# A GLA / S5 trunk on one core: GpSimd's elementwise work moved to VectorE, Toeplitz blocks read from the kernel table, low halves of the output weights by accumulating DMA

## The chip, the cores and the metric

The kernel runs on one core of a Trainium2 chip. The metric is device microseconds (us) of one execution. Five engines run their own instruction queues in order: TensorE (PE; its weight loads are shown as PEld), VectorE (DVE), ScalarE (ACT), GpSimd (POOL) and SyncE (SP), which here only issues DMAs. They meet through semaphores.

## The reference, cut to what matters

Two layers over x (512 tokens by 1024), each `x <- x + Mixer(RMSNorm(x))`, all in float32:

```
layer 0, GLA:  q,k,v,z,r = h @ w_in ; 4 heads, chunked, decay from sigmoid(r @ w_gate_up + b)
               o = attention inside the chunks + running state
               out = (rmsnorm_head(o) * silu(z)) @ w_out
layer 1, S5:   u,z = h @ w_in ; 128 groups of 16 channels, 64 complex states per group
               lam_bar = exp(lam*dt), b_bar = (lam_bar-1)/lam * b ; x_t = lam_bar*x_(t-1) + b_bar u_t
               y = gelu(Re(C x) + d*u) ; y = y*sigmoid(y @ w_glu + b_glu) * silu(z) ; out = y @ w_out
final RMSNorm
```

What S5's matrices hold is computed on the chip: for every group the powers of `lam_bar`, `b_bar` and C give a block Bm (inputs of 8 steps into the state), a block Cm (state into 8 outputs), a table E that rotates the states, and the short kernel K[0..7] (16 by 16 each), from which a lower Toeplitz block of 8 by 8 taps per group is laid out.

## The kernel before, in words

Every dense product is done in three matmuls on a high and a low half: weight and activation are split into `hi` (rounded for the fast fp32 mode) and `lo = value - hi`, and `three` adds hi*hi, hi*lo and lo*hi. A weight unit is 128 partitions by 1024 floats (512 KB); 136 units pass through the kernel, each feeding 24 matmuls of 128x512. `wunit` (L178) makes one unit. SP loads `raw` (two buffers, tag wraw). Then, of eight buffers of tag whl, four pairs, one pair is filled in one of two ways:

- plain: ACT copies raw to `hi` (L161), and DVE, or POOL where the table `UNITP` says so, subtracts (L162);
- with `dma=True`: ACT copies raw to `hi` (L185) and minus raw, rounded, to `lo` (L186), and POOL issues a DMA that adds the weight from HBM to `lo` (L187). It is used for w_z, w_qk and w_v of heads 1 to 3. w_out goes the plain way, all 16 units on DVE.

The GLA layer runs head by head (loop at L637). Of head h: `proj_qk`, then a weave of `proj_v`, `proj_out` of the head before (w_out) and `proj_z`, with the attention's steps `scores`, `state` and `mix` put between the units. Beside it runs S5Prep, which computes S5's matrices for 16 blocks of 8 groups. Its steps are called by `hook` from a list `plan`, at a pace `RATES`, each put off by `LOWS[step]` places of priority:

- F (`compute`, L1285): on POOL, ten elementwise operations per block: L1293, L1302 and L1304 on 128x1024, L1294 to L1297 on 128x512, L1309 to L1311 on 128x128 (and their inputs `lp`, `bb`, `xc`, `pp` loaded by SP, L1276 to L1282); then on DVE z = z + z2 (L1323) and the split of Bm into two fp16 halves (L1317 on ACT, L1318 on DVE), stored to HBM (L1319);
- Z (`finish_z`, L1326): the same split for Cm (z); PE computes the short kernel from z and bh (L1333); ACT and DVE evacuate (L1337, L1339), POOL adds the skip term and splits to fp16 (L1342 to L1345); SP stores it to the table `kz` in HBM (L1346); then `gcopy` (L1349) copies the block two before from `kz`, with overlapping strides, to the expanded Toeplitz matrix `gmd` (HBM to HBM, 512 KB);
- E (`etab`, L1250): a table by six operations on 128x512, the first three tables on DVE, the last five on POOL; G: the last `gcopy`.

S5's layer (L721 on) takes for each block sT, sR, sA, sB, sC and s5, scheduled by the tables TS to SGS, between the weight units of `win` (w_u, w_z, first of w_glu). `load_a` and `load_b` fetch Bm, E, the Toeplitz block and Cm with one DMA each (two each for the first three blocks). In sA POOL multiplies the scan's result (L812), in s5 POOL multiplies the gate with y (L847). 39 weight units there are plain, 23 of them subtracted on POOL. The last stretch, three quarters of w_glu and all of w_out of S5, is plain on ACT and DVE.

A scheduler builds each engine's queue from these priorities with its own estimate of durations; at run time each queue is strictly in order.

## Time and profile before

| | us |
|---|---|
| three runs | 1053.78, 1055.71, 1055.98 (median 1055.71) |
| profiled execution | 1054.56 |
| its span, first to last instruction | 1052.9 |
| PE busy | 927.6 (88%) |
| DVE busy | 713.8 (68%) |
| POOL busy | 511.0 (49%) |
| ACT busy | 472.2 (45%) |

The 1.7 us between span and time lie outside of the instructions. The busy share of an engine is an average over four stretches that differ: start and head 0 (to about 150 us), heads 1 to 3 with S5Prep beside them (150 to 550), S5 blocks between weight units (550 to 800), and weight units alone (from 800). A stretch is read by its own row. "Granted clock" (PEclk) is TensorE's clock as a share of full speed.

### The profile page before, as it was taken

To read this page: it belongs to the slowest core of one execution; us is meant where nothing else is said; L and a number is where in the kernel's file an instruction comes from. 1 tells how busy PE (TensorE), PEld (TensorE's weight loads), DVE (VectorE), ACT (ScalarE), POOL (GpSimd) and SP (SyncE) were. 2 spreads that over 40 slices of the span, in tenths; PEclk is the share of its full clock that TensorE was granted. 3 is DMA by queue.
4 is the path that set the end of the run, shared out by engine and by line. 5 is a ranking of instruction groups with operands and counts; after the bars stand their busy time and mean duration, and the time that the engine had idled before them with its cause. 6 is when DMAs were issued, how large, how long until landed. Compare 5 with 4: busy or idle time off the path is not lost. (4 is left out here: it accounts for less than half of the span.)

```text
span 1052.9 us, 13715 instructions
## 1 busy us (share of the span) xinstructions
PE 927.6 (88%) x5019; PEld 720.8 (68%) x5019; DVE 713.8 (68%) x916; ACT 472.2 (45%) x707; POOL 511.0 (49%) x477
## 2 busy tenths in 40 slices
PE   6795966699869796969989999999998999999996
PEld 5573754457646684747777777787777888888885
DVE  5794569957898887978645769789897432424322
ACT  5553343445546455433556684744453332313222
...
GB/s 256 221 183 100 87 167 185 276 247 262 265 209 250 228 292 273 237 321 317 190 226 259 151 121 250 211 300 252 264 185 140 110 82 99 100 160 100 100 61 80
DMA packets 118707, 205.79 MB, mean 195 GB/s; under 512 B 32400, under 2 KB 69824, under 8 KB 118640
## 3 DMA queue, kind: packets, MB, share of 16 engines
...
HBM read 167.69 MB, written 45.59 MB: 203 GB/s over the span
## 5 line engine op out<-in xcount | busy, mean ns | idle before, releaser
L162 DVE TENSOR_TENSOR whl<-wraw,whl 128x1024 fp32r<-128x1024 f32 x77 | 106.6, 1384 | 147.5 <-ACT whl L161 147.3
L161 ACT CAST whl<-wraw 128x1024 fp32r<-128x1024 f32 x100 | 104.7, 1048 | 183.7 <-PE pt L199 46.0
L202 PE MATMUL pd<-whl,actA 128*128 128x512 f32 x384 | 154.6, 408 | 12.9 <-ACT whl L161 9.2
L203 PE MATMUL pd<-whl,actA 128*128 128x512 f32 x384 | 154.2, 402 | 0.0
L204 PE MATMUL pd<-whl,actA 128*128 128x512 f32 x384 | 154.0, 404 | 0.0
L270 POOL TENSOR_TENSOR rstd<-rv,neghalf 128x1 f32<-128x1 f32 (+1 forms) x6 | 5.2, 874 | 248.4 <-DVE rv L269 248.4
L198 PE MATMUL pd<-actA,whl 128*128 128x512 f32 x256 | 101.6, 403 | 3.3 <-ACT u L732 3.1
L200 PE MATMUL pd<-actA,whl 128*128 128x512 f32 x256 | 101.4, 397 | 0.0
L202 PEld LDWEIGHTS pd<-whl,actA 128*128 128x128 f32 x384 | 74.4, 194 | 32.7 <-ACT whl L161 9.2
L202 PE MATMUL pd<-whl,q 128*128 128x512 f32 x192 | 80.3, 419 | 11.7 <-DVE xx L541 5.1
L204 PEld LDWEIGHTS pd<-whl,actA 128*128 128x128 f32 x384 | 73.9, 193 | 18.6 <-issue 2.8
L203 PEld LDWEIGHTS pd<-whl,actA 128*128 128x128 f32 x384 | 73.9, 192 | 17.7 <-issue 2.1
L162 POOL TENSOR_TENSOR whl<-wraw,whl 128x1024 fp32r<-128x1024 f32 x23 | 58.3, 2533 | 52.5 <-ACT whl L161 49.2
L203 PE MATMUL pd<-whl,q 128*128 128x512 f32 x192 | 79.6, 415 | 0.0
L1318 DVE TENSOR_TENSOR q<-q,q 128x1024 f16<-128x1024 f32 x32 | 60.4, 1886 | 12.6 <-ACT q L1317 12.3
L198 PEld LDWEIGHTS pd<-actA,whl 128*128 128x128 f32 x256 | 48.5, 190 | 16.6 <-ACT u L732 5.2
L1293 POOL TENSOR_TENSOR q<-q,q 128x1024 f32<-128x1024 f32 x16 | 43.4, 2709 | 31.7 <-DMA q<-s_bi 29.6
L198 PE MATMUL po<-actA,whl 128*128 128x512 f32 x128 | 52.4, 409 | 5.8 <-ACT whl L185 5.8
L185 ACT CAST whl<-wraw 128x1024 fp32r<-128x1024 f32 x36 | 37.7, 1046 | 44.0 <-PE pd L203 26.4
L200 PEld LDWEIGHTS pd<-actA,whl 128*128 128x128 f32 x256 | 48.4, 189 | 11.2
L204 PE MATMUL pd<-whl,q 128*128 128x512 f32 x128 | 53.7, 424 | 1.4 <-DVE q L165 1.4
L202 PEld LDWEIGHTS pd<-whl,q 128*128 128x128 f32 x192 | 38.4, 200 | 23.6 <-DVE xx L541 6.4
...
## 6 DMA issues: line engine op xcount, KB each, us to landing
wraw<-w_glu SPq DMA_DIRECT2D x32, 512.0 KB, 3.4
wraw<-w_v SPq DMA_DIRECT2D x16, 512.0 KB, 5.4
wraw<-w_z SPq DMA_DIRECT2D x16, 512.0 KB, 6.5
whl<-w_z POOLq DMA_DIRECT2D x16, 512.0 KB, 7.9
wraw<-w_out SPq DMA_DIRECT2D x16, 512.0 KB, 6.8
q<-lpt SPq DMA_DIRECT2D x16, 512.0 KB, 6.8
q<-s_bi SPq DMA_DIRECT2D x16, 512.0 KB, 9.5
...
```

The costliest lines, as they stand in the source:

```text
L161: i0 = A.copy(out=dst_hi, in_=src)
L162: i1 = E.tensor_tensor(out=dst_lo, in0=src, in1=f(dst_hi), op=SUB)
L185: A.copy(out=hi, in_=raw)
L198: PE.matmul(acc, lhsT=wh, rhs=ah, start=first, stop=False)
L200: mark["pe"] = PE.matmul(acc, lhsT=wl, rhs=ah, start=False, stop=last).ins
L202: PE.matmul(acc, lhsT=ah, rhs=wh, start=first, stop=False)
L203: PE.matmul(acc, lhsT=ah, rhs=wl, start=False, stop=False)
L204: mark["pe"] = PE.matmul(acc, lhsT=al, rhs=wh, start=False, stop=last).ins
L270: G.tensor_tensor(out=dst, in0=v, in1=neghalf.to_broadcast([P, w]), op=ALU.pow)
L1293: tt(out=m, in0=lp, in1=bb, op=MUL)
L1318: nc.vector.tensor_tensor(out=hl[:, 1], in0=src, in1=hl[:, 0], op=SUB)
```

## The change

Three things, and two tables that go with them (`LOWS`: F 0 to 30, Z 20 to 30; `UNITP` and `EV` are gone).

1. All elementwise work of POOL named above goes to DVE: `compute`, the end of `finish_z`, `etab`, L812, L847 and the 23 subtractions of weight units. On POOL stay the set-up (`small`), 16 small memsets of sR, the powers of RMSNorm and the DMA issues.
2. `gcopy` and `gmd` are gone. A Toeplitz block is read by eight DMAs, one per group (`toep`), each of 16x8 rows of 512 bytes, straight from `kz`.
3. w_out of the GLA layer is loaded with `dma=True`.

```diff
-LOWS = {'F': 0, 'Z': 20, 'E': 100, 'G': 0}
+LOWS = {'F': 30, 'Z': 30, 'E': 100}
...
-            E = V
-            if pool:
-                E = G if UNITP[wcnt[0]] else V
-                wcnt[0] += 1
-            mark["act"], mark["dve"] = split(hi, lo, raw, E=E)
+            mark["act"], mark["dve"] = split(hi, lo, raw)
...
-            yield from dense_tok(w_out[h, n], o[0], o[1], ev, per_tb=True)
+            yield from dense_tok(w_out[h, n], o[0], o[1], ev, per_tb=True, dma=True)
...
+        if src is prep.kz:
+            for g in range(GB):
+                S.dma_start(out=w[g // 4][:, g % 4 * 2 * P:(g % 4 + 1) * 2 * P], in_=prep.toep(cb * GB + g))
...
-        G.tensor_tensor(out=t1, in0=sh, in1=co, op=MUL)
+        V.tensor_tensor(out=t1, in0=sh, in1=co, op=MUL)
...
-        G.tensor_tensor(out=sz[cb], in0=sz[cb], in1=yv[cb], op=MUL)
+        V.tensor_tensor(out=sz[cb], in0=sz[cb], in1=yv[cb], op=MUL)
...
     def etab(self, ck):
-        tt = (nc.vector if ck < EV else nc.gpsimd).tensor_tensor
+        tt = nc.vector.tensor_tensor
...
     def compute(self, cb):
-        G = self.nc.gpsimd
-        tt = G.tensor_tensor
+        tt = self.nc.vector.tensor_tensor
...
-        G.tensor_tensor(out=dk, in0=self.dm, in1=self.kd[:, cb:cb + 1].to_broadcast([P, 16]), op=MUL)
-        G.tensor_tensor(out=ke[:, 0:16], in0=ke[:, 0:16], in1=dk, op=ADD)
-        G.tensor_copy(out=kf[:, :, 0], in_=ke)
-        G.tensor_tensor(out=kf[:, :, 1], in0=ke, in1=kf[:, :, 0], op=SUB)
+        V.tensor_tensor(out=dk, in0=self.dm, in1=self.kd[:, cb:cb + 1].to_broadcast([P, 16]), op=MUL)
+        V.tensor_tensor(out=ke[:, 0:16], in0=ke[:, 0:16], in1=dk, op=ADD)
+        V.tensor_copy(out=kf[:, :, 0], in_=ke)
+        V.tensor_tensor(out=kf[:, :, 1], in0=ke, in1=kf[:, :, 0], op=SUB)
...
-    def gcopy(self, cb):
-        src = bass.AP(self.kz.tensor, self.kz[cb * GB].offset + 7 * 32, [[2 * KW, P], [-32, T], [1, 2 * P]])
-        self.nc.sync.dma_start(out=self.gmd[cb].rearrange("g (i j) w -> (g i) j w", j=T), in_=src)
+    def toep(self, g):
+        return bass.AP(self.kz.tensor, self.kz[g].offset + 7 * 32, [[2 * KW, 16], [-32, T], [1, 2 * P]])
```

Lines of the changed kernel stand 3 to 19 lower (L1285 `compute` is L1273 on, L1333 is L1320, L161 in `split` is L158 and L164 is L161). How the queues come out of the scheduler is seen at three places.

First, ACT's queue at the start of head 1 in the kernel before. whl are weight tiles (here w_out), big_1230 to big_1233 the four token blocks of v, which the next state and mix matmuls on PE read, q_246 the first Bm:

```order
L161 CAST big_1277<-pt_1273 128x128
L164 ACTIVATE q_199_1188<-pt_1183,hgp 128x128 x2
L161 CAST big_1329<-pt_1325 128x128
L161 CAST whl_1524<-wraw_1522 128x1024
L161 CAST whl_1605<-wraw_1603 128x1024
L161 CAST big_1338<-pt_1334 128x128
L164 ACTIVATE big_1230<-pd_1238,rstd_77_513 128x512
L164 ACTIVATE big_1231<-pd_1239,rstd_77_513 128x512
L164 ACTIVATE big_1232<-pd_1240,rstd_77_513 128x512
L164 ACTIVATE big_1233<-pd_1241,rstd_77_513 128x512
L161 CAST whl_1675<-wraw_1673 128x1024
L1317 CAST q_246_1387<-q_205_1206 128x1024
```

The same place in the changed kernel, where big_1229 and the following are v:

```order
L180 CAST whl_1606<-wraw_1604 128x1024
L181 ACTIVATE whl_1607<-wraw_1604 128x1024
L161 ACTIVATE q_199_1187<-pt_1182,hgp 128x128
L158 CAST big_1276<-pt_1272 128x128
L180 CAST whl_1677<-wraw_1675 128x1024
L181 ACTIVATE whl_1678<-wraw_1675 128x1024
L161 ACTIVATE q_199_1187<-pt_1182,hgp 128x128 x2
L158 CAST big_1328<-pt_1324 128x128
L1304 CAST q_261_1450<-q_207_1212 128x1024
L158 CAST big_1337<-pt_1333 128x128
L161 ACTIVATE big_1229<-pd_1237,rstd_77_512 128x512
L161 ACTIVATE big_1230<-pd_1238,rstd_77_512 128x512
```

In the kernel before, the second and third units of w_out stand ahead of v; in the changed one all four do, with two operations each (the first two units stand a few rows above this piece, with q_246's cast), and two casts of S5Prep.

Second, DVE's queue at the end of head 1's gate projection (L396 and L398 gate the head's output, tile big; L433 and L438 belong to the next head's decay), before:

```order
L396 SCALAR_TENSOR_TENSOR tmp_1962<-tmp_1962,pd_1739 128x512
L398 SCALAR_TENSOR_TENSOR big_1556<-tmp_1958,rsv_1843,big_1556 128x512
L396 SCALAR_TENSOR_TENSOR tmp_1966<-tmp_1966,pd_1740 128x512
L398 SCALAR_TENSOR_TENSOR big_1579<-tmp_1962,rsv_1843,big_1579 128x512
L398 SCALAR_TENSOR_TENSOR big_1710<-tmp_1966,rsv_1843,big_1710 128x512
L433 TENSOR_SCALAR tmp_1976<-pt_1974,bg 128x512
L396 SCALAR_TENSOR_TENSOR tmp_1970<-tmp_1970,pd_1741 128x512
```

and in the changed kernel, where L386 and L388 are those operations and L1281 to L1289 are `compute`:

```order
L386 SCALAR_TENSOR_TENSOR tmp_1963<-tmp_1963,pd_1741 128x512
L1281 TENSOR_TENSOR q_412_2153<-q_413_2154 128x8x64
L1289 TENSOR_TENSOR q_414_2160<-big_1953,pp_1954 128x1024
L388 SCALAR_TENSOR_TENSOR big_1557<-tmp_1959,rsv_1845,big_1557 128x512
L386 SCALAR_TENSOR_TENSOR tmp_1967<-tmp_1967,pd_1742 128x512
L388 SCALAR_TENSOR_TENSOR big_1580<-tmp_1963,rsv_1845,big_1580 128x512
L1282 TENSOR_TENSOR q_413_2154<-q_368_1951,q_369_1952 128x8x64
L1283 TENSOR_TENSOR q_413_2154<-q_368_1951,q_369_1952 128x8x64
```

Operations of `compute` now stand one or two at a time between those of the head.

Third, SP's queue where S5 loads a block (number 4 of 16), before:

```order
L581 DMA q_1017_5268<-bmd 128x2048
L581 DMA q_1018_5270<-tab 128x1024
L581 DMA q_1019_5272<-gmd 128x8x256
L581 DMA q_1020_5274<-cmd 128x2048
```

and in the changed kernel:

```order
L570 DMA q_1017_5285<-bmd 128x2048
L570 DMA q_1018_5287<-tab 128x1024
L565 DMA q_1019_5289<-kz 128x1x256 x8
L570 DMA q_1020_5298<-cmd 128x2048
```

One DMA has become eight.

## Rows read from the trace of the kernel before

**Rows 1.** Stretches: start:end and length, each engine's busy us (x instructions), PEclk, DMA, GB/s.
```profile
150.00:550.00 400.00, 329.21 (x1413) 245.39 (x1413) 322.00 (x333) 187.53 (x296) 336.51 (x285) 0.90 0.88 253
550.00:800.00 250.00, 234.51 (x1997) 188.29 (x1996) 204.46 (x250) 137.74 (x192) 96.99 (x66) 0.98 0.68 218
800.00:1053.00 253.00, 244.21 (x1111) 196.40 (x1110) 90.08 (x106) 74.52 (x101) 8.97 (x8) 0.99 0.32 100
```

**Rows 2.** Two shorter stretches, the same columns.
```profile
700.00:750.00 50.00, 47.00 (x455) 38.37 (x454) 47.80 (x53) 20.52 (x30) 20.79 (x18) 1.00 0.81 261
850.00:1025.00 175.00, 175.00 (x754) 140.93 (x752) 59.37 (x64) 49.68 (x63) 0.00 (x0) 1.00 0.33 103
```

**Rows 3.** Waits of PE, 150 to 550 us: sum, times, longest.
```profile
PE pt L1333 <- DVE q L1323: 12.3, 2, 6.5
PE pt L1333 <- POOL bh L1311: 7.6, 2, 5.4
```

**Rows 4.** DVE's groups by form, 150 to 550 us.
```profile
L1318 DVE TENSOR_TENSOR q<-q,q 128x1024 f16<-128x1024 f32 x32 | 60.4, 1886 | 12.6 <-ACT q L1317 12.3
L162 DVE TENSOR_TENSOR whl<-wraw,whl 128x1024 fp32r<-128x1024 f32 x18 | 33.4, 1857 | 11.2 <-ACT whl L161 11.2
L1323 DVE TENSOR_TENSOR q<-q,q 128x1024 f32<-128x1024 f32 x16 | 30.2, 1891 | 0.0
L398 DVE SCALAR_TENSOR_TENSOR big<-tmp,rsv,big 128x512 f32<-128x512 f32 x12 | 24.1, 2038 | 0.0
L541 DVE TENSOR_TENSOR xx<-pd,xx 128x512 f32<-128x512 f32 x32 | 21.7, 680 | 4.4 <-PE pd L204 4.4
L174 DVE SCALAR_TENSOR_TENSOR big<-big,ges,big 128x512 fp32r<-128x512 f32 x9 | 18.5, 2052 | 0.1
L535 DVE TENSOR_TENSOR rsv<-rsv,rstd 128x4 f32<-128x4 f32 x3 | 11.2, 3749 | 3.1 <-POOL rsv L270 3.1
```

**Rows 5.** DVE's groups by form, 850 to 1025 us.
```profile
L162 DVE TENSOR_TENSOR whl<-wraw,whl 128x1024 fp32r<-128x1024 f32 x32 | 39.2, 1226 | 115.9 <-ACT whl L161 115.9
```

**Rows 6.** DVE in order of time: start, us, operation.
```profile
148.98 0.28 DVE L171 TENSOR_TENSOR big<-att,big 128x128 fp32r<-128x128 f32 x1
...
151.20 0.69 DVE L1260 TENSOR_TENSOR q<-big,big 128x512 f32<-128x512 f32 x1
151.80 0.68 DVE L1263 TENSOR_TENSOR q<-big,big 128x512 f32<-128x512 f32 x1
```

**Rows 7.** POOL's groups by form, 150 to 550 us.
```profile
L1293 POOL TENSOR_TENSOR q<-q,q 128x1024 f32<-128x1024 f32 x16 | 43.4, 2709 | 31.7 <-DMA q<-s_bi 29.6 <-issue 1.7 <-DMA tab<-q 0.4
L1297 POOL TENSOR_TENSOR q<-q 128x512 f32<-128x512 f32 x16 | 27.4, 1710 | 0.1
L1311 POOL TENSOR_TENSOR bh<-bh,bh 128x128 f32<-128x128 f32 x16 | 14.7, 920 | 0.1
```

**Rows 8.** The accumulating DMAs (L187): issue min/median/max ns, then landing us.
```profile
L187 POOL DMA_DIRECT2D whl<-w_v x12: 866/894/1948, 87.4 to 386.9; - x12
...
DMA to landing us min/median/max: 5.3/7.9/11.9
```

**Rows 9.** ACT in order of time at the start of head 1.
```profile
159.24 1.04 ACT L161 CAST whl<-wraw 128x1024 fp32r<-128x1024 f32 x1 [8.48 <-DMA wraw<-w_out]
...
162.53 2.43 ACT L164 ACTIVATE big<-pd,rstd 128x512 fp32r<-128x512 f32 x4
```

**Rows 10.** PE in order of time at the start of head 1.
```profile
163.28 1.22 PE L202 MATMUL po<-big,big 128*128 128x512 f32 x2 [11.08 <-ACT big L164]
169.34 0.80 PE L202 MATMUL pd<-whl,q 128*128 128x512 f32 x1 [4.84 <-DVE big L165]
```

**Rows 11.** SP's issues in order of time there.
```profile
118.24 0.33 SPq L180 DMA_DIRECT2D wraw<-w_out  x1
...
144.75 4.63 SPq L966 DMA_DIRECT2D kz<-tmp  x9
...
152.38 0.85 SPq L180 DMA_DIRECT2D wraw<-w_out  x2
```

**Rows 12.** DMAs: KB each, median us from issue to landing.
```profile
wraw<-w_out SPq DMA_DIRECT2D x16, 512.0 KB, 6.8
q<-gmd SPq DMA_DIRECT2D x13, 512.0 KB, 5.3
kz<-tmp SPq DMA_DIRECT2D x16, 56.0 KB, 1.9
```

More of the change, by code (lines that the diff above doesn't have):

```diff
@@ L58 @@
 LOW1, LOW2 = 20, 0
-EV = 3
 SCP = -20
@@ L157, in trunk_kernel, with split @@
     mark = {}
-    def split(dst_hi, dst_lo, src, scale=None, E=V):
+    def split(dst_hi, dst_lo, src, scale=None):
         if scale is None:
             i0 = A.copy(out=dst_hi, in_=src)
-            i1 = E.tensor_tensor(out=dst_lo, in0=src, in1=f(dst_hi), op=SUB)
+            i1 = V.tensor_tensor(out=dst_lo, in0=src, in1=f(dst_hi), op=SUB)
         else:
@@ L204, in three, with dense_tok @@
             mark["pe"] = PE.matmul(acc, lhsT=al, rhs=wh, start=False, stop=last).ins
-    def dense_tok(w, ah, al, evac, per_tb=False, late=True, major=1, pool=False, banks=None, dma=False):
+    def dense_tok(w, ah, al, evac, per_tb=False, late=True, major=1, banks=None, dma=False):
         nkb = 4 if per_tb else len(ah)
@@ L222, in fetch @@
         def fetch(u):
-            return wunit(w[u], 2, 512, pool=pool, dma=dma)
+            return wunit(w[u], 2, 512, dma=dma)
         for u in range(nu - major + 1):
@@ L245, in dense_tok, with dense_ch @@
                 yield
-    def dense_ch(w, ah, al, evac, pool=False, banks=None):
+    def dense_ch(w, ah, al, evac, banks=None):
         nkb = len(ah)
@@ L250, in dense_ch @@
         for u in range(nkb // 2):
-            hi, lo = wunit(w[u], 2, 512, pool)
+            hi, lo = wunit(w[u], 2, 512)
             for m in range(4):
@@ L364, in trunk_kernel @@
             ne += 1
-    plan.append(("G", NB - 1))
     pace = [0.0]
@@ L567, in loadw @@
         n = 1024 if dt == F16 else 512
-        if src is prep.gmd:
-            srcs = [src[cb, 4 * k:4 * k + 4].rearrange("g p w -> p g w") for k in range(2)]
-            full = src[cb].rearrange("g p w -> p g w")
-        else:
-            srcs = [src[cb][:, k * n:(k + 1) * n] for k in range(2)]
-            full = src[cb]
-        fit = (lambda t: t.rearrange("p (g w) -> p g w", w=2 * P)) if src is prep.gmd else (lambda t: t)
         if cb < NPRE:
             w = [T_([P, n], "big", BIG, dt) for _ in range(2)]
-            for k in range(2):
-                S.dma_start(out=fit(w[k]), in_=srcs[k])
-            return w
-        t = q4(dt, 2 * n)
-        S.dma_start(out=fit(t), in_=full)
-        return [t[:, :n], t[:, n:]]
+        else:
+            t = q4(dt, 2 * n)
+            w = [t[:, :n], t[:, n:]]
+        if src is prep.kz:
+            for g in range(GB):
+                S.dma_start(out=w[g // 4][:, g % 4 * 2 * P:(g % 4 + 1) * 2 * P], in_=prep.toep(cb * GB + g))
+        elif cb < NPRE:
+            for k in range(2):
+                S.dma_start(out=w[k], in_=src[cb][:, k * n:(k + 1) * n])
+        else:
+            S.dma_start(out=t, in_=src[cb])
+        return w
     def wsel(w):
@@ L597, in load_b @@
         t = st_[cb]
-        t["gh"] = gsel(loadw(cb, prep.gmd))
+        t["gh"] = gsel(loadw(cb, prep.kz))
         t["cm"] = wsel(loadw(cb, prep.cmd))
@@ L866, in win @@
             if c[0] == "u":
-                yield from dense_tok(s_wu[n], h2, l2, lambda tb, acc, n=n: ev_u(n, tb, acc), late=False, pool=True)
+                yield from dense_tok(s_wu[n], h2, l2, lambda tb, acc, n=n: ev_u(n, tb, acc), late=False)
             elif c[0] == "z":
-                yield from dense_ch(s_wz[n], h2, l2, lambda m, acc, n=n: ev_z(4 * n + m, acc), pool=True)
+                yield from dense_ch(s_wz[n], h2, l2, lambda m, acc, n=n: ev_z(4 * n + m, acc))
             else:
-                yield from dense_ch(w_glu[n], yh, yl, lambda m, acc, n=n: ev_g(4 * n + m, acc), pool=True)
+                yield from dense_ch(w_glu[n], yh, yl, lambda m, acc, n=n: ev_g(4 * n + m, acc))
     jobs = {}
@@ L948, in __init__ @@
         self.cmd = dr.tile([NB, P, 2 * GB * P], F16, name="cmd")
-        self.gmd = dr.tile([NB, GB, P, 2 * P], F16, name="gmd")
         self.tab = dr.tile([NB, P, 2 * GB * NC], F32, name="tab")
```

10 lines of the change are left out of this document (1 added, 9 removed).

## The prediction

> **What bounds the kernel now.** I read the table of stretches first, looking in each for the engine that is hardly ever idle [rows 1]. From 800 us on PE works 244.2 of 253 us and POOL 9.0; the change finds next to nothing there. From 550 to 800 PE works 234.5 of 250, so 15.5 us are all that can be won. From 150 to 550 PE works 329.2 of 400: 70.8 us idle, with DVE at 322.0 (80.5%) and POOL at 336.5 (84%). The granted clock there is 0.90, against 0.98 and 0.99 later. So the change is decided in heads 1 to 3 with S5Prep beside them; before 150 us it touches little.
>
> Second, PE's waits there. No single one carries the idle time. Two go back to S5Prep's chain: the short-kernel matmul waits 12.3 us for DVE and 7.6 for POOL [rows 3]. The longest pair is at the start of head 1, 11.08 + 4.84 = 15.9 us [rows 10]: PE wants v from ACT, and ACT had waited 8.48 us for a raw unit of w_out before it came to v's splits at 162.53 [rows 9]. SP had issued that raw load only at 152.38, behind nine small stores [rows 11].
>
> Third, DVE's groups. An operation on two 128x1024 inputs in SBUF takes 1226 ns where POOL does nothing [rows 5] and 1857 to 1891 ns where POOL is at work; the three-input 128x512 ones take 2038 and 2052, and a 128x4 one 3749. L541, with one input in PSUM, takes 680, like a free 128x512 record of 0.69 [rows 4, 6]. So DVE's 322 us hold much time in which it waits for POOL.
>
> **DVE in the 150 to 550 stretch.** What goes: POOL's elementwise work, and with it the stretching. From [rows 4] less the free prices: 32 x (1.886 - 1.226) = 21.1; 18 x (1.857 - 1.226) = 11.4; 16 x (1.891 - 1.226) = 10.6; 12 x (2.038 - 0.69) = 16.2; 9 x (2.052 - 0.69) = 12.3; 3 x (3.749 - 0.28) = 10.4, with 0.28 for a small record [rows 6]. Together 82. Smaller groups must have some too; I take 100, within 82 and 120 (an estimate).
>
> The w_out subtractions leave DVE: 16 x 1.14 = 18. Here and below I count operations back to back: 128x512 records of 0.69 start 0.60 apart [rows 6], so 0.09 overlaps; that makes 1.14 of 1.226, and 0.20 of 0.28.
>
> What comes: F, per block three operations of 1.14, four of 0.60 and three of 0.20, 6.4 us, x16 = 103. Four small ones of `finish_z`, 0.8, x15 = 12. E, five tables of six operations, 30 x 0.60 = 18. Four weight units, 4.6. Together 137.
>
> DVE then has 322 + 137 - 18 - 100 = 341 us, 85% of 400 (321 to 360 by the bounds). What took POOL 2709, 1710 and 920 ns an operation [rows 7], 336.5 / 16 = 21 us per block with all else [rows 1], takes DVE 1.14, 0.60 and 0.20, some 8. How full can DVE run before it sets the pace? Between 700 and 750 it was busy 47.8 of 50 us, 95.6%, while PE worked 47.0 [rows 2]; at that use 341 us fit into 357. At today's 80.5% they need 424.
>
> **First term, PE's waits from 150 to 550.** Without the start of head 1 (the second term) 70.8 - 15.9 = 54.9 us are idle. What hangs on POOL (19.9 of [rows 3], and DVE operations that are a microsecond late because of it) should go; what hangs on ACT and on PE's own chains stays. I take half: -27. Bounds: -55 (all goes) and +24 (DVE keeps today's use, 424 - 400).
>
> PE's own busy time could shrink as well if the granted clock rose from 0.90 to the 0.98 of the next stretch: 329.2 x (1 - 0.90/0.98) = 27 us at most. I leave it out of the term, since a stretch with half of the waits left would not have it.
>
> **Second term, the start of head 1.** In ACT's queue all four units of w_out, two operations each, and two of S5Prep's casts now stand ahead of v's split, where two units stood. One unit's ACT work is 2 x 1.04 [rows 9]; the raw tile has only two buffers, and a load lands 6.8 us after issue [rows 12]. The first raw load was issued at 118.24 and the next at 152.38 [rows 11], so the third unit's raw still lands at about 159; the fourth needs its buffer freed by ACT's second operation on the unit two before. v's split, at 162.53 before, then comes 3 to 11 us later: +7. Bounds: -5, should SP issue earlier without POOL's chain ahead of it, and +11.
>
> **Third term, 550 to 800.** DVE takes over POOL's 97.0 us. At free prices these are 19 subtractions at 1.14 and some 16 products and 16 gates at about 0.7 (between the two spacings above), about 44 us; relief of the stretched ones takes back 23 to 35 (estimates by the same difference, 1.86 - 1.23 for each). DVE: 204.5 + 44 - 23 to 35 = 214 to 225 of 250, 86 to 90%, under the 95.6% at which PE still ran. 0, within -10 (two thirds of the idle 15.5) and +12.
>
> The Toeplitz blocks: nine zero stores take 4.63 us of SP, 0.51 each [rows 11], so eight issues take 4.1 us where one took about 0.5: +3.6 per block, x13 blocks in this stretch = 47 of 250 us. SP has that: most of its time it waits for buffers, and its loads run ahead. What else lies in its queue behind the eight is Cm and the next raw weight, 3.6 us later. If that cover is gone it is 3.6 us per block, at most 47. In exchange SP no longer issues the 16 copies to `gmd`, nor waits for `kz` ahead of them. A piece of 56 KB lands in 1.9 us and 512 KB in 5.3 [rows 12]; eight side by side should be there within 4.1 + 1.9 = 6.0.
>
> [...]
>
> **w_out by accumulation, no term of its own.** ACT gets 16 x 1.04 = 17 us more (187.5 to 204 of 400). The hi/lo pair is held for ACT 2.1, issue 0.9, landing 7.9 [rows 8] and PE's 24 matmuls, 24 x 175.0/754 = 5.6 [rows 2]: 16.5 us, with four pairs one unit in 4.1 us, faster than PE's 5.6. With the worst issue and landing, 2.1 + 1.95 + 11.9 + 5.6 = 21.5, 5.4 per unit, just hidden. The cover is gone only when raw comes late: + 6.8 is 28.3, or 7.1 per unit, 1.5 us on each.
>
> The issues in [rows 8] run from 866 to 1948 ns. [...]
>
> **Sum.** -27 + 7 + 0 = -20 against the profiled execution, 1054.56: 1034.6. That execution is 1.15 us below the median of the three runs (1055.71). I forecast 1035 us; its own range is 1015 to 1050.
>
> **Rivals.**
> B. Nearly all of the 54.9 us go, and the clock recovers with them. For it: DVE's minimum of 357 us leaves 43, and half of the clock's 27 is 13: -43 - 13 = -56, about 1000. Against it: it asks 95.6% of DVE among many short chains.
> C. No net change. POOL was slack: only 19.9 us of PE's waits name S5Prep, and those [rows 3] are waits of a matmul whose place the scheduler now sets later. The gain at them (some -7) meets the +7 at the start of head 1: 1055.
> D. Slower, by DVE's one queue. The three operations of `compute` that now stand between L386 and L388 of the head, and others like them, hold up the gate, the states and the evacuations that PE waits for; POOL had a queue of its own for them. From the point at which DVE cannot be used above 85% (its 341 us in 400) it costs time; at the 80.5% of today, 424 - 400 = +24: 1079. For it: a queue with 341 us of work from two chains. Against: [rows 2].
> E. The weights come late, by SP's eight issues or by the accumulation. Half of the 47 us, or 1.5 us on 16 units, take the forecast's gain back: 1035 + 10 to 35, 1045 to 1070.
>
> **How the numbers follow.** Forecast 0.45, B 0.15, C 0.15, D 0.15, E 0.10. The three runs of before span 0.2% (2 us), about what a measurement of this kernel can tell from no change. Faster: 0.44 of the forecast, all of B, half of E's and a fifth of C's: 0.44 + 0.15 + 0.05 + 0.03 = 0.67. Same: 0.01 + 0.06 of C = 0.07. Slower: D, the rest of C and of E: 0.26. The range cuts B's lower half and D's upper half: 1005 to 1066.
>
> **What would show it.** Right: the 128x1024 subtraction of the Bm split falls from 1886 to about 1230 ns and L388 from 2038 to about 700; DVE is busy 335 to 360 us between 150 us and the end of the GLA layer; PE's waits at L1320 (the short kernel) lose most of 19.9; the gap before head 1's first state matmul grows from 11.08 to 14 or more. The third term is right if PE's idle time in S5's blocks stays between 6 and 27 us and PE waits there for no tile loaded at L565. The step most likely to fail is "half of the waits": if PE's idle time between 150 us and the end of GLA is above 65 us with DVE under 85% full, the waits were chains that POOL had no part in (C); if it is with DVE above 85%, it is D. If the DVE groups stay at 1.8 us, POOL was not what stretched them, and the whole working falls: DVE would have 441 us of work, and the kernel would be over 40 us slower.

## The result, and the profile after

The changed kernel takes 1065.24 us (median of 8 runs, 1060.30 to 1070.38), the kernel before on the same chips 1055.85: ratio 1.0092, 95% interval 1.0065 to 1.0120. It is slower by some 9 us where 1035 us, faster, had been forecast. The profiled execution took 1063.15 us, its span is 1061.4.

The cut that tells most is the point at which PE has transposed the last block of x1, the input of the S5 layer: 523.2 us in the kernel before, 522.8 after. Both programs have executed the same matmuls there; below, what lies before it is called the GLA half and what lies behind it the S5 half. Columns as in [rows 1]; first the kernel before:

```profile
0.00:523.20 523.20, 424.74 (x1796) 316.67 (x1797) 406.33 (x542) 245.52 (x390) 384.72 (x386) 0.91 0.83 230
523.20:1052.90 529.70, 502.88 (x3225) 404.17 (x3223) 307.50 (x375) 226.68 (x318) 126.31 (x92) 0.98 0.51 162
```

and after:

```profile
0.00:522.80 522.80, 424.08 (x1796) 315.03 (x1797) 388.02 (x771) 259.96 (x410) 109.18 (x163) 0.90 0.85 233
522.80:1061.40 538.60, 506.54 (x3224) 405.97 (x3222) 309.85 (x440) 225.99 (x315) 5.78 (x22) 0.97 0.50 156
```

In the GLA half PE is idle for 523.2 - 424.7 = 98.5 us before and 98.7 after: 275 us of POOL are gone, and PE does not notice. In these two executions the whole loss is in the second half: 538.6 against 529.7, of which 5.2 us are idle time and 3.7 PE's longer busy time at a lower granted clock (0.97 against 0.98). One execution of each tells the place only roughly: two executions of one program below (e3 and e13) differ by 8.4 us in the GLA half.

What was to happen on DVE did happen. Its groups of 150 to 550 us, to be held against [rows 4] (the Bm and Cm split, z + z2, the gate, the state, the 128x4 product, then the two products that had been L1293 and L1302 on POOL, [rows 7]):

```profile
L1305 DVE TENSOR_TENSOR q<-q,q 128x1024 f16<-128x1024 f32 x32 | 38.7, 1216 | 15.7 <-ACT q L1304 15.7
L1310 DVE TENSOR_TENSOR q<-q,q 128x1024 f32<-128x1024 f32 x16 | 19.5, 1217 | 0.1
L388 DVE SCALAR_TENSOR_TENSOR big<-tmp,rsv,big 128x512 f32<-128x512 f32 x12 | 8.7, 742 | 0.0
L171 DVE SCALAR_TENSOR_TENSOR big<-big,ges,big 128x512 fp32r<-128x512 f32 x9 | 6.7, 741 | 0.0
L525 DVE TENSOR_TENSOR rsv<-rsv,rstd 128x4 f32<-128x4 f32 x3 | 0.5, 156 | 0.9 <-POOL rsv L261 0.9
L1280 DVE TENSOR_TENSOR q<-q,q 128x1024 f32<-128x1024 f32 x16 | 19.5, 1219 | 14.7 <-DMA q<-s_bi 14.7
L1289 DVE TENSOR_TENSOR q<-big,pp 128x1024 f32<-128x1024 f32 x16 | 19.5, 1220 | 12.6 <-DMA big<-s_xc 7.9 <-DMA pp<-pw 3.3 <-issue 1.5
```

1886 ns became 1216, 2038 became 742, 3749 became 156. But look at the last column of the last two rows: DVE now stands still for 14.7 and 12.6 us before products whose inputs are loads of S5Prep (14.7 and 11.2 of it for DMAs). In the kernel before that wait stood in POOL's queue (29.6 us in [rows 7]), and most of it was a single wait, for the first block:

```profile
156.28 2.34 POOL L1293 TENSOR_TENSOR q<-q,q 128x1024 f32<-128x1024 f32 x1 [27.56 <-DMA q<-s_bi]
```

Of the heads, that queue held only the issues of accumulating DMAs and the powers of RMSNorm; the splits of q and the gates were in DVE's. The stretch's row, against [rows 1]:

```profile
150.00:550.00 400.00, 329.65 (x1418) 244.23 (x1419) 310.08 (x577) 204.16 (x319) 43.36 (x49) 0.88 0.89 253
```

DVE is busy 310 of 400 us, 77.5%, and so not full. PE is idle for 70.4 us there, 70.8 before. Its waits have changed their place and hardly their sum. At the scores, the matmuls of q and k at a head's start (L493 before, L483 after), it waited 7.3 us before and waits 30.0 after (sum, times, longest):

```profile
PE pt L493 <- DVE big L162: 3.6, 1, 3.6
PE pt L493 <- DVE q L165: 2.3, 2, 1.7
PE pt L493 <- DVE tmp L1339: 1.4, 2, 0.7
```
```profile
PE pt L483 <- DVE q L162: 13.7, 3, 7.5
PE pt L483 <- DVE big L159: 11.5, 2, 11.0
PE pt L483 <- DVE tmp L1326: 4.8, 2, 4.1
```

At the short kernel (L1333 before, L1320 after) its waits fell only from 20.3 to 12.4 us.

**The start of head 1.** DVE in order of time (in brackets the idle time before, and what ended it):

```profile
145.01 0.60 DVE L162 SCALAR_TENSOR_TENSOR q<-pt,hgp,q 128x128 fp32r<-128x128 f32 x2
150.88 1.23 DVE L1280 TENSOR_TENSOR q<-q,q 128x1024 f32<-128x1024 f32 x1 [5.26 <-DMA q<-s_bi]
152.02 0.60 DVE L162 SCALAR_TENSOR_TENSOR q<-pt,hgp,q 128x128 fp32r<-128x128 f32 x2
...
173.45 0.35 DVE L162 SCALAR_TENSOR_TENSOR q<-pt,hgp,q 128x128 fp32r<-128x128 f32 x1 [3.37 <-ACT q L161]
```

ACT, where the last of w_out's four raw units is late and a split of q stands behind it:

```profile
171.16 1.04 ACT L180 CAST whl<-wraw 128x1024 fp32r<-128x1024 f32 x1 [8.44 <-DMA wraw<-w_out]
172.11 1.05 ACT L181 ACTIVATE whl<-wraw 128x1024 fp32r<-128x1024 f32 x1
173.06 0.35 ACT L161 ACTIVATE q<-pt,hgp 128x128 fp32r<-128x128 f32 x1
...
179.74 1.27 ACT L161 ACTIVATE big<-pd,rstd 128x512 fp32r<-128x512 f32 x2
```

and PE, which wants those splits:

```profile
152.42 1.11 PE L398 MATMUL pt<-ident,big 128*128 128x128 f32 x4 [7.12 <-DVE q L162]
168.94 0.80 PE L483 MATMUL pt<-big,big 128*128 128x128 f32 x2 [11.00 <-DVE big L159]
177.45 0.80 PE L483 MATMUL pt<-big,big 128*128 128x128 f32 x2 [7.50 <-DVE q L162]
...
182.48 1.22 PE L193 MATMUL po<-big,big 128*128 128x512 f32 x2
```

L162 at 152.02 had its inputs early; it waited because L1280 stood ahead of it in the queue and L1280 waited for a DMA. Behind it come many more operations of S5Prep: from 146 us to the first state matmul DVE executes 31 of them, 5 in the kernel before. From 143 to 190 us PE is busy 12.8 us, before 27.0. v's split on ACT starts at 179.74, against 162.53 in [rows 9], and the first state matmul of head 1 at 182.48, against 163.28 in [rows 10]. The accumulating w_out is not what it takes for that: in e13 below, which loads w_out the plain way, that matmul comes later still.

```profile
186.61 1.22 PE L193 MATMUL po<-big,big 128*128 128x512 f32 x2 [3.70 <-ACT big L161]
```

**SP's queue.** Late in the GLA half, and in S5:

```profile
474.29 5.76 SPq L565 DMA_DIRECT2D big<-kz  x7
480.15 1.01 SPq L568 DMA_DIRECT2D big<-cmd  x2
481.26 0.85 SPq L175 DMA_DIRECT2D wraw<-w_out  x2
...
742.70 6.93 SPq L565 DMA_DIRECT2D q<-kz  x8
749.74 0.52 SPq L175 DMA_DIRECT2D wraw<-w_glu  x1
```

The eight issues at 742.70 take 6.93 us, the twelve rows of eight in this trace 5.0 to 8.8, not the 4.1 that nine zero stores had led me to expect [rows 11], and raw weights are the next in the queue. For w_out that is paid at once: ACT's cast waits 11.80 us for it and PE 10.45 (ACT and PE, in order of time). In e2 (below; w_out plain) PE waits 4.41 us at this place, in e3 and e13, with one load per block, 0.23.

```profile
487.39 1.04 ACT L180 CAST whl<-wraw 128x1024 fp32r<-128x1024 f32 x1 [11.80 <-DMA wraw<-w_out]
```
```profile
492.54 0.79 PE L193 MATMUL pd<-whl,q 128*128 128x512 f32 x1 [10.45 <-ACT q L161]
```

In S5 it is not the raw weights that come later: from 530 us on ACT waits 17.6 us for them, before 22.4. What it waits longer for is y, the output of an S5 block, which SP reads back from HBM in the same queue as the eight issues: 24.0 us against 15.4 before. With eight issues on SP it is 21.6 in e2 and 21.7 in e17, without them 15.6 in e13, 17.4 in e3 and 12.6 in e5; but e4 has 11.1 with them and e18 19.9 without. That PE's time hangs on this wait is not shown.

The accumulating issues themselves are calmer than in [rows 8]: w_v's take at most 1251 ns instead of 1948, and w_out's a mean of 872 on a POOL with little else to do.

```profile
L182 POOL DMA_DIRECT2D whl<-w_out x16 | 14.0, 872 | 120.8 <-ACT whl L181 65.3 <-ACT q L161 51.4 <-ACT tmp L1324 4.0
```

### The profile page after: what moved, and what is told of

Same layout as the page of the kernel before. It is cut to its first block, busy times and chain, and to the rows that moved or that the text cites. A ratio compares the mean times of both kernels' runs of the same rounds, so it can differ in the third digit from the quotient of the medians.

```text
span 1061.4 us, 13671 instructions
## 1 busy us (share of the span) xinstructions
PE 930.6 (88%) x5019; PEld 721.0 (68%) x5019; DVE 697.9 (66%) x1209; ACT 485.9 (46%) x723; POOL 115.0 (11%) x184
## 4 chain that ended last, share of the span: by engine, by line
PE 57%; DMA 16%; DVE 12%; ACT 9%; issue 3%; SPq 2%; POOL 0%; ACTq 0%; POOLq 0%; DVEq 0%
PE pd L193 7%; PE pd L194 7%; PE pd L195 7%; PE pd L190 5%; PE pd L189 5%; PE pd L191 5%; DMA big<-s_xc 4%; ACT u L721 3%; DMA q<-s_bi 3%; DMA wraw<-w_out 2%; PE po L190 2%; PE po L189 2%; PE po L191 2%; PE pt L190 1%; PE po L193 1%
## 5 line engine op out<-in xcount | busy, mean ns | idle before, releaser
L159 DVE TENSOR_TENSOR whl<-wraw,whl 128x1024 fp32r<-128x1024 f32 x84 | 102.6, 1223 | 160.6 <-ACT whl L158 158.9
L158 ACT CAST whl<-wraw 128x1024 fp32r<-128x1024 f32 x84 | 88.1, 1050 | 172.0 <-PE pd L190 43.9
L193 PE MATMUL pd<-whl,actA 128*128 128x512 f32 x384 | 152.8, 403 | 14.9 <-ACT whl L158 9.6
L194 PE MATMUL pd<-whl,actA 128*128 128x512 f32 x384 | 153.4, 399 | 0.7 <-DMA whl<-w_v 0.7
L195 PE MATMUL pd<-whl,actA 128*128 128x512 f32 x384 | 151.4, 399 | 0.0
L189 PE MATMUL pd<-actA,whl 128*128 128x512 f32 x256 | 103.5, 411 | 10.7 <-DVE tmp L746 5.8
L191 PE MATMUL pd<-actA,whl 128*128 128x512 f32 x256 | 102.3, 402 | 0.0
L193 PEld LDWEIGHTS pd<-whl,actA 128*128 128x128 f32 x384 | 73.1, 191 | 33.6 <-ACT whl L158 9.6
L193 PE MATMUL pd<-whl,q 128*128 128x512 f32 x192 | 79.1, 416 | 16.6 <-ACT q L161 10.4
L194 PEld LDWEIGHTS pd<-whl,actA 128*128 128x128 f32 x384 | 73.1, 190 | 18.5 <-issue 2.1
L195 PEld LDWEIGHTS pd<-whl,actA 128*128 128x128 f32 x384 | 72.9, 190 | 17.1 <-issue 2.0
L194 PE MATMUL pd<-whl,q 128*128 128x512 f32 x192 | 78.2, 409 | 0.0
L181 ACT ACTIVATE whl<-wraw 128x1024 fp32r<-128x1024 f32 x52 | 54.9, 1056 | 10.8 <-DMA etd<-tmp 10.8
L191 PEld LDWEIGHTS pd<-actA,whl 128*128 128x128 f32 x256 | 49.5, 193 | 11.2
L193 PEld LDWEIGHTS pd<-whl,q 128*128 128x128 f32 x192 | 38.0, 198 | 27.5 <-ACT q L161 10.9
L189 PE MATMUL po<-actA,whl 128*128 128x512 f32 x128 | 51.4, 402 | 4.3 <-ACT whl L180 4.3
L195 PE MATMUL pd<-whl,q 128*128 128x512 f32 x128 | 52.2, 417 | 0.0
L190 PE MATMUL pd<-actA,whl 128*128 128x512 f32 x128 | 52.1, 407 | 0.0
L721 ACT ACTIVATE u<-pd,rsP 64x256 f32<-64x256 f32 x64 | 47.8, 747 | 7.5 <-DVE mxr L714 3.4
L191 PE MATMUL po<-actA,whl 128*128 128x512 f32 x128 | 50.0, 393 | 1.0 <-DMA whl<-w_qk 1.0
```

The source lines that it names most:

```text
L158: i0 = A.copy(out=dst_hi, in_=src)
L159: i1 = V.tensor_tensor(out=dst_lo, in0=src, in1=f(dst_hi), op=SUB)
L181: mark["act"] = A.activation(out=lo, in_=raw, func=AF.Copy, scale=-1.0).ins
L189: PE.matmul(acc, lhsT=wh, rhs=ah, start=first, stop=False)
L190: PE.matmul(acc, lhsT=wh, rhs=al, start=False, stop=False)
L191: mark["pe"] = PE.matmul(acc, lhsT=wl, rhs=ah, start=False, stop=last).ins
```

## The experiments

All ratios are to the kernel before, timed beside the kernel on the same chip. "First part" below is POOL's elementwise work on DVE with the priorities F 30 and Z 30; "second" the eight Toeplitz DMAs; "third" w_out by accumulation.

| run | kernel | median us | ratio (95% interval) |
|---|---|---|---|
| | all three parts | 1065.24 | 1.0092 (1.0065 to 1.0120) |
| e1 | first + third | 1058.63 | 1.0037 (1.0007 to 1.0067) |
| e2 | first + second | 1056.42 | 1.0000 (0.9974 to 1.0026) |
| e3 | first | 1045.49 | 0.9891 (0.9852 to 0.9930) |
| e13 | first, another chip | 1043.97 | 0.9907 (0.9873 to 0.9941) |
| e4 | second | 1063.42 | 1.0068 (1.0031 to 1.0106) |
| e5 | e2, Toeplitz issued by POOL | 1050.53 | 0.9948 (0.9918 to 0.9978) |
| e17 | first, copy kept, its load cut in eight | 1047.73 | 0.9948 (0.9918 to 0.9979) |
| e6 | first, one more ACT pass on w_out | 1055.61 | 1.0011 (0.9983 to 1.0039) |
| e7 | first, one more DMA of w_out (4 runs) | 1076.95 | 1.0205 (1.0154 to 1.0256) |
| e12 | first + third, minus pass on DVE | 1056.35 | 1.0008 (0.9976 to 1.0039) |
| e8 | first, S5Prep's loads from POOL | 1056.20 | 1.0036 (1.0012 to 1.0059) |
| e9 | first, zero stores from POOL | 1050.07 | 0.9975 (0.9944 to 1.0007) |
| e10 | first, S5Prep three steps later | 1052.25 | 0.9991 (0.9959 to 1.0023) |
| e16 | first, no S5Prep steps at heads' starts | 1051.82 | 0.9989 (0.9963 to 1.0014) |
| e14 | first, one load per block left out | 1050.54 | 0.9967 (0.9937 to 0.9997) |
| e15 | before, the same load left out | 1059.21 | 1.0058 (1.0026 to 1.0090) |
| e11 | first, but S5's own work left on POOL | 1054.46 | 0.9994 (0.9964 to 1.0024) |
| e18 | first, priorities as before | 1050.96 | 0.9964 (0.9931 to 0.9996) |

### Part by part: e1 to e4, e13

The edits are pieces of the change undone: e1 takes the second part back, e2 the third, e3 both; e4 is the kernel before with the second alone.

```diff
 e1, e3
-            for g in range(GB):
-                S.dma_start(out=w[g // 4][...], in_=prep.toep(cb * GB + g))
+        S.dma_start(out=fit(t), in_=src[cb]...)   # gmd, and gcopy in finish_z's step
 e2, e3
-            ... dense_tok(w_out[h, n], o[0], o[1], ev, per_tb=True, dma=True)
+            ... dense_tok(w_out[h, n], o[0], o[1], ev, per_tb=True)
```

> The changed kernel with the expanded Toeplitz matrix back: HBM-to-HBM copies, then one load per block in place of eight. Theory S (SP's queue): in the changed kernel eight issues for one block took 5.8 to 8.8 us of SP, and a raw weight of w_out issued behind them kept ACT waiting 11.8 us and PE 10.45 at 482 us; without them that gap goes, and some 10 us come back: 1050 to 1057. Theory D (VectorE's queue now waits for DMAs that GpSimd used to wait for): nothing of it changes here, 1062 to 1068.

> The changed kernel with w_out loaded the plain way (ACT casts, VectorE subtracts). Theory A (ACT's queue at the start of head 1: four units of w_out with two operations each stand ahead of the splits of q and v; ACT waits 8.44 us there for a raw unit and PE 7.4 of them): one operation on ACT per unit, the order of queues changes back in part, and 5 to 10 us come back: 1055 to 1060. Theory D: the gaps at 145 to 170 us are VectorE's waits for the inputs of S5's preparation (5.26 and 2.11 us) and stay: 1062 to 1068; 16 more subtractions on VectorE cost up to 5 more.

> Only the first part of the change: GpSimd's elementwise work on VectorE, with the Toeplitz copy and the plain w_out of before. If the first part is the gain that was forecast and the other two lost it: 1030 to 1045. Theory D (the waits for DMAs moved onto VectorE's queue take back what the end of the contention gives): 1053 to 1063.

> The kernel before with only the eight Toeplitz DMAs in place of the copy and the one load. Theory S: 3.6 to 6 us of SP more per block delay weights; 1060 to 1068. If SP's slack hides them, and the copies' traffic was the dearer part: 1050 to 1056.

> Only the first part, the same program as before, on this chip. If its gain is real: 1042 to 1048, ratio 0.985 to 0.993. If it was one chip's: 1050 to 1056.

The first part alone gains 10.6 us, on two chips: less than the forecast's 20, but its sign. The second part costs 10.9 us on top of it (e2 less e3), 6.6 on top of first and third, 7.3 on top of the kernel before. The third costs 13.1 (e1 less e3), or 8.8 on top of first and second. So the parts roughly add up, and the two that the prediction put at nothing turn the gain around. Where each of them costs is less clear. A profiled execution can lie far from its median (e3's is 7.3 us below, e4's 6.7 below, e1's 7.0 above, e13's 5.1 above), and the halves, cut as in the section on the result, with PE's idle time in brackets, are:

| run | profiled us | GLA half | S5 half |
|---|---|---|---|
| before | 1054.56 | 523.2 (98.5) | 529.7 (26.8) |
| all three | 1063.15 | 522.8 (98.7) | 538.6 (32.1) |
| e3, first | 1038.22 | 511.4 (94.8) | 525.1 (21.0) |
| e13, first | 1049.08 | 519.8 (98.0) | 527.6 (22.3) |
| e2, first + second | 1056.52 | 518.0 (95.6) | 536.8 (31.8) |
| e1, first + third | 1065.67 | 528.2 (110.3) | 535.8 (27.3) |
| e4, second | 1056.74 | 529.7 (102.4) | 525.3 (25.6) |

The S5 halves of e2, e13 and e1:

```profile
518.00:1054.80 536.80, 505.02 (x3224) 403.48 (x3222) 310.38 (x438) 224.16 (x310) 5.75 (x22) 0.97 0.50 156
```
```profile
519.80:1047.40 527.60, 505.27 (x3225) 403.95 (x3223) 309.21 (x436) 224.26 (x310) 6.73 (x22) 0.98 0.50 160
```
```profile
528.20:1064.00 535.80, 508.48 (x3231) 406.33 (x3230) 312.37 (x441) 225.92 (x314) 5.80 (x22) 0.98 0.50 160
```

With the same PE work the S5 half of e2 is 9.2 us longer than that of e13, and all of it is idle time (31.8 against 22.3 us). That speaks for S5 as the place of the second part's cost; but e1, which lacks the second part, is almost as long there, and e4, which has it, is not. The third part shows as idle time in the GLA half of e1 (110.3 us) and not in that of the changed kernel (98.7). So the prices are measured, and their places are not settled.

### What the Toeplitz DMAs cost: e5, e17

```diff
 e5 (from e2)
-                S.dma_start(out=w[g // 4][...], in_=prep.toep(cb * GB + g))
+                G.dma_start(out=w[g // 4][...], in_=prep.toep(cb * GB + g))
 e17 (from e3)
-        S.dma_start(out=fit(t), in_=full)
+            for g in range(GB):
+                S.dma_start(out=t[:, g * 2 * P:(g + 1) * 2 * P], in_=src[cb, g])
```

> First and second part of the change (VectorE does GpSimd's work, Toeplitz blocks straight from the table, plain w_out), with the eight Toeplitz DMAs issued from GpSimd's queue, which has next to nothing else to do. Against 1056.4 with SP issuing them and 1045.5 with the copy. Theory S (what costs is SP's one queue: eight issues of 0.7 to 1.1 us, with weights behind them): most of the 11 us comes back, 1044 to 1050. Rival T (what costs are the small transfers themselves or the order of the other queues): 1054 to 1060.

> Only the first part (copies to the expanded Toeplitz matrix kept), with the one load per block cut into eight from the fourth block on, all on SP. Theory S (SP's queue: eight issues of some 0.6 to 1.1 us, two raw weights right behind them): 5 to 10 us over the 1044 to 1045 of the first part alone, and the S5 blocks take 298 to 306 us instead of 294 to 296. Rival (the removed copies, or what the smaller pieces from the table cost): within 3 us.

Both sides come out in between: issuing from POOL gives back 0.52% of the 1.09% that the second part cost, and eight issues with the copy kept cost 0.4 to 0.6% over e3 and e13. Both fit the view that about half of the price is SP's time for the issues, and e17's contiguous pieces are slow to issue too, 3.64 to 7.20 us for eight from 700 to 740 us, where those from the table took 6.79 to 9.21 in e2:

```profile
704.24 7.20 SPq L574 DMA_DIRECT2D q<-gmd  x8
711.54 0.38 SPq L175 DMA_DIRECT2D wraw<-s_wz  x1
```

It is not shown, though: neither difference is larger than what a mere change of priorities costs below (e18, 0.6 to 0.7%), and e17's 0.4% against e13 lies within the intervals. What the other half is, is not settled either.

### What the accumulating w_out costs: e6, e7, e12

```diff
 e6 (from e3)
+                A.activation(out=lo, in_=raw, func=AF.Copy, scale=-1.0)   # overwritten by DVE
 e7 (from e3)
+                G.dma_start(out=lo.rearrange(...), in_=src)               # overwritten by DVE
 e12 (from e1)
-                mark["act"] = A.activation(out=lo, in_=raw, func=AF.Copy, scale=-1.0).ins
+                mark["dve"] = V.tensor_scalar(out=lo, in0=raw, scalar1=-1.0, scalar2=None, op0=MUL).ins
```

> Only the first part, and for each of the 16 units of w_out one more pass of ACT over the unit (minus raw into the low tile, which VectorE then overwrites): ACT's share of the accumulating way without its DMA. Against 1045.5 without the pass and 1058.6 with the accumulating way. Theory A (ACT's queue: two operations per unit ahead of the splits of q and v): 1053 to 1059. Rival M (the accumulating DMA: 8 MB more in a stretch whose DMA engines are 0.89 busy, and its landing of 8 to 9 us): 1044 to 1049.

> Only the first part, and for each unit of w_out one more DMA of the unit from GpSimd's queue into the low tile, which VectorE then overwrites: the accumulating way's transfer and its landing without ACT's second pass. Against 1045.5 without it. Rival M: 1053 to 1060. Theory A: 1044 to 1049.

> First and third part (accumulating w_out, the copy back), but minus the weight is made by VectorE, one operation with a single input, in place of ACT's second pass. Against 1058.6 with ACT's pass and 1045.5 with the plain way. Theory A (ACT's second pass ahead of the splits of q and v): 1045 to 1051. Theory M (the accumulating DMA and its landing): 1055 to 1061.

ACT's second pass alone costs 10 to 13 us, which speaks for the queue of ACT; yet taking that pass off ACT saves next to nothing (1.0008 against 1.0037, the intervals overlap), and a plain DMA of the same bytes costs 31 us or more. The effects do not add up to one cause: each half alone costs as much as both, or more. One thing goes with most of them: ACT's waits for raw units of w_out, 14.2 and 14.5 us in e3 and e13, are 23.2 in e6, 35.6 in e7, 30.0 in e12 and 27.5 in the changed kernel; but in e1 they are 14.7. That the third part costs 9 to 13 us is measured; its mechanism stays open.

### Where PE's idle time in the GLA half goes: e8, e9, e10, e16, e14, e15

```diff
 e8:  S5Prep.load:      S = self.nc.sync        ->  S = self.nc.gpsimd
 e9:  S5Prep.zero:      self.nc.sync.dma_start  ->  self.nc.gpsimd.dma_start
 e10: pace = [0.0] -> [-2.52];  RATES 0.84, 0.84, 0.88 -> 0.92, 0.92, 0.92
 e16: QZ = [2, 3] -> [0, 3];    RATES 0.84 ... 0.94 -> 0.98, 0.98, 1.0, 1.0, 1.0
 e14, e15: load: the DMA of bb (s_bi) left out, a tile on the chip in its place
```

> Only the first part, with the four loads per block of S5's preparation issued from GpSimd's queue in place of SP's. Theory D (VectorE's queue stands still while a product waits for a load that SP issued late behind other waits; 1.3 to 5.3 us at a time, some 30 us in the changed kernel): the loads come earlier, VectorE's waits for them fall to under half and the time to 1034 to 1042. Rival: the loads are late because their buffers come free late, on whichever queue: 1043 to 1049.

> Only the first part, and the sixteen zero stores to the kernel table issued from GpSimd's queue. In SP's queue ten of them (6.0 us) stand right ahead of the loads of S5's first block and of w_out at the start of head 1. Theory D: there VectorE waits 5.8 us for the first block's input with the splits of q behind it, ACT 7.2 and 3.4 us for w_out, and PE is idle for 36 us where it was idle 16 in the kernel before; with the loads earlier PE's idle time from 143 to 190 us falls below 26 us and the time to 1030 to 1038. Rival: the operations of S5's preparation that fill VectorE's queue there cost the time, whenever their inputs come: idle time 32 to 38 us, 1042 to 1048.

> Only the first part, with S5's preparation started three steps later and run at a pace of 0.92 in place of 0.84 to 0.88, so that it ends at the same place. The loads of w_out then stand ahead of the second block's loads, and half as many operations of the preparation stand between the splits of q and the scores at the start of head 1. Theory D2 (the preparation's operations in VectorE's queue among head 1's cost the time there, by their number): idle time of PE from 143 to 190 us at 20 to 28 us instead of 36, 1032 to 1040. Theory D (only the waits for loads cost): 32 us or more of idle time, as the first block's input comes as late as ever; 1043 to 1048.

> Only the first part, without the two steps of the preparation that the program puts at the start of each head, between the q projection and the scores; the pace is 0.98 to 1.0 instead, so that the preparation ends at the same place. Theory D2 (the preparation's operations in VectorE's queue at the heads' starts cost): PE's idle time up to the first state matmul of head 1 falls from 62 to under 50 us without coming back at head 2, 1030 to 1040. Rival (the work comes back elsewhere, as with the later start, where it came back as 15.6 us at the start of head 2): 1045 to 1053.

> Only the first part, with one of the two 512 KB loads per block of S5's preparation left out (B's columns are replaced by a tile that is on the chip): 16 loads, 8.4 MB, and the wait that VectorE's queue has for them (24.9 us of its waits in heads 1 to 3) are gone; the operations stay. Theory D (VectorE's queue waits for loads, with the heads' operations behind): 10 to 20 us less than the first part alone, and more than the kernel before gains by the same edit. Theory M (the DMA engines, 0.89 busy, are the limit): as much less in both. Rival: nothing, since the next load is as late: within 4 us.

> The kernel before with the same load left out. Theory D: GpSimd's queue waited for it, 29.6 us in all, and nothing of the heads stood behind; 0 to 5 us less than before. Theory M: 10 to 20 us less.

From 143 to 190 us, e13 (the first part), then e9, e10 and e16, one fence each:

```profile
143.00:190.00 47.00, 10.91 (x41) 6.50 (x40) 40.96 (x76) 14.04 (x26) 0.00 (x0) 0.57 0.74 222
```
```profile
143.00:190.00 47.00, 23.80 (x88) 17.34 (x89) 40.98 (x81) 15.50 (x28) 0.00 (x0) 0.66 0.73 216
```
```profile
143.00:190.00 47.00, 29.01 (x107) 22.17 (x106) 37.01 (x71) 17.78 (x32) 1.77 (x2) 0.71 0.60 172
```
```profile
143.00:190.00 47.00, 30.15 (x115) 22.33 (x114) 38.60 (x74) 17.90 (x32) 1.77 (x2) 0.75 0.66 185
```

Locally the idle time of PE falls each time, from 36.1 to 23.2, 18.0 and 16.9 us (the kernel before has 20.0 there, not the 16 of e9's expectation), and the first state matmul of head 1 moves from 186.61 to 180.22, 167.35 and 167.22. That parts two readings of the start of head 1: the wait of DVE's queue for the first load, and the number of S5Prep's operations that stand there among the head's. The wait is as long in e10 as in e13 (DVE in e13, then DVE and PE in e10):

```profile
152.30 1.22 DVE L1283 TENSOR_TENSOR q<-q,q 128x1024 f32<-128x1024 f32 x1 [6.00 <-DMA q<-s_bi]
```
```profile
153.06 1.23 DVE L1283 TENSOR_TENSOR q<-q,q 128x1024 f32<-128x1024 f32 x1 [6.82 <-DMA q<-s_bi]
```
```profile
167.35 1.20 PE L193 MATMUL po<-big,big 128*128 128x512 f32 x2
```

What differs is the number: from 146 us to that matmul DVE executes 37 operations of S5Prep in e13, 30 in e9, 6 in e10 and 6 in e16. So what costs there is mainly the number (theory D2 of e10's expectation); the wait, some 6 us, is in all of them.

The time does not fall: all three are slower than the first part as it is. Much of the idle time comes back elsewhere in the half. In e10 that is seen at the start of head 2:

```profile
287.73 1.08 PE L1323 MATMUL pt<-q,bh 128*32 128x256 f32 x8 [15.64 <-DVE q L162]
```

Over the whole GLA half PE is idle 94.8 and 98.0 us in e3 and e13, 90.8 in e9, 96.1 in e10, 93.4 in e16, 93.1 in e18, and 98.5 in the kernel before. The rows of e9 and e16:

```profile
0.00:512.40 512.40, 421.65 (x1789) 315.27 (x1790) 401.36 (x785) 245.37 (x396) 101.48 (x163) 0.91 0.83 234
```
```profile
0.00:521.80 521.80, 428.45 (x1796) 317.32 (x1797) 406.22 (x790) 247.88 (x398) 94.69 (x146) 0.91 0.82 232
```

So a repair that takes 13 to 19 us of idle time from one place takes at most some 7 from the whole half. In e9 and e16 no single wait of PE later in the half stands out as in e10. Nor does the GLA half explain the time: in e9's execution it is as short as in e3's, and the S5 half longer (532.0 us against 525.1). e8 is a miss of its own: with the loads on another queue, DVE's waits for DMAs fall only from 41 us (e3) to 32, and PE waits 2.4 us for an accumulation (w_v) that now shares that queue.

e14 and e15 fit neither theory. With 8.4 MB of loads left out, the first part is 6 to 8 us slower than with them (0.9967 against 0.9891 and 0.9907), and the kernel before is 6 us slower too. Less work made both programs slower. Of e14's rival, that the next load is as late, the trace shows something: DVE's waits for the load are gone, but those for the other loads grow, and all its waits for DMAs from 118 to 560 us fall only from 45.4 us (e13) to 32.5. In both runs the scheduler also gave DVE's queue another order, in e14 from 144 us on. Which of this costs the time is not shown.

### S5's own work, and how much another order makes: e11, e18

```diff
 e11: G.tensor_tensor for the product after the scan, the gate and UNITP's subtractions, as before
 e18: LOWS = {'F': 30, 'Z': 30, ...}  ->  {'F': 0, 'Z': 20, ...}
```

> Only the first part, but with the S5 layer's own work (the product after the scan, the gate, 23 subtractions of weights) left on GpSimd; the preparation and the tables stay on VectorE. If the gain of the first part comes from heads 1 to 3 alone: 1043 to 1048. If the S5 layer's share is worth something, as half of GpSimd's operations there go and VectorE's are relieved: 1050 to 1054. If it costs, as its operations stand in VectorE's one queue: 1036 to 1042.

> Only the first part, with the priorities of the preparation's steps as before the change (F 0, Z 20 in place of 30 and 30). If any other order of the queues costs as much as the second and third part did: 1049 to 1056. If the first part's gain does not hang on this table: 1042 to 1048.

e18 changes no instruction of any engine, only the priorities that the change had moved as well. DVE's queue has another order from 186 us on, and the kernel is 6 to 8 us slower than the first part (0.9964 against 0.9891 and 0.9907). The difference of 0.6 to 0.7% has an uncertainty of some 0.5% (an estimate from the intervals), so it is clear of noise, but only just.

e11 is more than another order. DVE's queue is that of e3 up to 496 us; what differs is S5's own work, which is back on POOL. That costs 9 to 11 us and leaves no gain over the kernel before (0.9994, 0.9964 to 1.0024); of its three expectations the one by which the S5 layer's share is worth something came nearest. So the preparation and the tables, moved to DVE by themselves, gain nothing that can be measured. The gain of the first part hangs on S5's own work on DVE, or on the order that goes with it; no run parts the two.

Eight relatives of the first part (e8 to e11, e14, e16 to e18) are all slower than it, by 0.4 to 1.5%, whatever they change. So some of its gain may be an order that happens to be good, and 6 to 8 us is what another order cost in the one test that changed nothing else. The 7 to 13 us of the second and third part lie at that size or just above.

## Why the prediction was wrong

The first step that failed is the first term, half of PE's waits gone, -27. It took PE's idle time to hang on POOL and thus to go with it. PE's idle time from 150 to 550 us stayed (70.8 to 70.4 us), and in the whole GLA half too (98.5 to 98.7). e11 tests the term almost alone, with the preparation on DVE and S5's own work on POOL: it gains nothing (0.9994). The prediction had named this outcome: above 65 us of idle time with DVE under 85% full, the waits were chains that POOL had no part in, its rival C. The rows add what C lacked: the waits that POOL left were made up for by new ones at the scores (7.3 to 30.0 us), at the start of head 1 behind S5Prep's operations in DVE's queue. That is the mechanism of rival D, at a DVE only 77.5% full, where D had put its start at 85%. At the start of head 1 it was the order of the queue that made PE wait, not its load.

DVE's relief, on which the term was built, was larger than taken: with 310 us busy where 322 + 137 - 18 = 441 would have stood, 131 us by the same sum, against 100. So 310 lies below the stated 321 to 360. The sum was right in sign and more, and it was not the quantity that mattered.

The second term was mis-sized and had the wrong engine. +7 was taken for ACT's casts ahead of v; v's split came 17.2 us later and the first state matmul 19.2, beyond the bound of +11. In e13, without the accumulating w_out, that matmul comes 23.3 us later, so the doubled casts are not needed for it. What the runs showed in its place is S5Prep in DVE's queue: with 6 of its operations there instead of 37 (e10, e16) the matmul comes 19 us earlier, though the first load keeps DVE waiting as long as before (6.0 to 6.8 us). That wait could have been read from [rows 7], where POOL's L1293 waited 29.6 us for the load, 27.6 of them until 156.28. I carried the durations over to DVE as a sum for the stretch, and left out the waits and the place at which the operations would stand.

The third term, 0 for the S5 blocks, failed at "SP has that". A block's issues took 5.0 to 8.8 us instead of 4.1, what stands behind them in the queue is issued later, and the second part costs 7 to 11 us. The sign that was to show the term right did not catch it: from 550 to 800 us PE is idle for 20.0 us, within the 6 to 27, and waits for no tile loaded at L565 (a weight load does once, 0.3 us), but it executed 1896 instructions there instead of 1997. Rival E had the two parts that cost, at a tenth of the chance, and gave 1045 to 1070, which holds the result; its mechanism is seen at one raw load of w_out (PE's 10.45 us), fits half of the second part's price, and is not shown for the rest. Eight loads of 64 KB in place of one of 512 KB, with the copies gone, cost 7.3 us in e4; that the price is SP's issue time is argued for half of it (e5, e17), and not shown.

"No term of its own" for w_out failed too: the ring of pairs was worked out as a flow, and by that estimate 4.1 us per unit are hidden behind PE's 5.6; what costs 9 to 13 us is not shown. Long issues on POOL, up to 1948 ns in [rows 8], were not seen for w_out: 872 ns on average and 912 at most, with DVE 77.5% busy.

Right were the stretching by POOL (1886 ns fell to 1216 and 2038 to 742, about the free prices) and that the last stretch would be untouched (8.8 us of PE's idle time from 800 us on, before and after). That the range, 1005 to 1066, held the time was luck: it held 1065.24 by 0.8 us, on the side away from the forecast and not by the forecast's mechanism.
